# A hybrid trunk's prompt layer summed inside the dense value stage, with paced gathers and another instruction order

## The chip, the cores and the metric

The kernel runs on one core of a Trainium2 chip. The metric is the device time of one execution in microseconds. A core has five engines, each with its own instruction stream: TensorE (PE, matmuls; PEld is its weight loading), VectorE (DVE), ScalarE (ACT), GpSimd (POOL) and SyncE (SP). They meet at semaphores only. SP issues the plain DMA transfers, POOL the indirect ones (gathers of table rows by index).

## What is computed

Two layers over two independent token groups: a prompt of 128 tokens (P, one tile of 128) and a sample of 512 tokens (S, four tiles). Width is 1024, all in float32. Each layer mixes tokens, normalizes, and then passes each token through PEER, a layer of 16384 experts of which every token uses 8 x 16:

```python
def _trunk(x, cvec, lru_state, wkv_state, P):
    for l in range(DEPTH):
        sh1, sc1, g1, sh2, sc2, g2 = _modulation(cvec, w_mod[l], b_mod[l])
        h = _layer_norm(x) * (1.0 + sc1) + sh1
        if l % 2 == 0:
            mix = concat([_fourier_mix(a_in), _short_conv_mix(b_g, c_g, x_in, ...)]) @ w_out_e
        else:
            mix = concat([_lru_mix(...), _rwkv_mix(...)]) @ w_out_o
        x = _layer_norm(ALPHA * x + g1 * mix, ln1)
        h2 = _layer_norm(x) * (1.0 + sc2) + sh2
        x = _layer_norm(ALPHA * x + g2 * _peer(h2, ...), ln2)

def _peer(h, wq, keys, u_tab, v_tab):
    idx, gate = top 16 of 16 x 16 product keys per head, 8 heads
    act = gelu(einsum('td,thkd->thk', h, u_tab[idx]))
    return einsum('thk,thkd->td', gate * act, v_tab[idx])
```

## The kernel before, in words

**The order of the work.** `build` runs layer 0 (`even_mixers`, then `S.peer_layer`) and layer 1 (`odd_mixers`, then `S.peer_layer`). The prompt's work is threaded into these four parts.

**PEER in two ways.** The sample's tiles 1 to 3 go through all 16384 experts as matmuls, in 128 chunks of 128 experts. `hidden` (L1245) multiplies a chunk of u by the tokens and takes the gelu. `dense_peer` (L1255), called the value stage here, multiplies that by the chunk's gates (L1276), splits it into two parts for full precision (`ah` on ACT at L1278, `al` on DVE at L1279), and adds its product with a chunk of v into PSUM (L1285: 18 matmuls a chunk; a chunk of `hidden` has 24, in the helper at L1079). Weight blocks are split likewise (`split`, L1219: the rounded half on ACT, L1222, the rest, `lw`, on DVE, L1224). 64 hidden chunks of a layer are computed ahead and spilled to DRAM while the tiles are routed, so that in the value stage 4 chunks of every 8 are hidden there and 4 are read back. The gates reach DRAM through `one_hot` (L1207) and `scatter_gates` (L1187).

The sample's tile 0 and the prompt's tile go by gathers: for each of 128 slots POOL fetches 128 rows of u (a tile of 512 KB, `gather`, L1145), DVE multiplies and sums them (L1138, a *dot*), then 128 slots of v are fetched and added up (L1168, an *add*). "Sum" below means either. Two tiles, two tables, two layers and 128 slots make 1024 gathers and as many sums.

**The queue.** These gathers are generators in `B.tasks`. `pump(n)` (L199) advances the first of them by n gathers. Others call it as they go: `split` pumps `B.rate`, `one_hot` 1, the value stage enough to be done by chunk 122, less `OVER` = 88 gathers in layer 0, which stay for the odd mixers. `pace(n, src)` (L222) puts a one-column POOL copy of `src` ahead of the gathers it pumps, so that they can't be issued before `src` is there. `defer` (L212) keeps two sums behind the latest gather. Buffers for gathered rows: 4, and 3 more from the pool of the value stage.

**The odd layer.** `odd_mixers` (L1487 and after) starts the sample's `odd_lora` (L608), then `run` (L1378) interleaves generators for the recurrent heads, at most 5 at a time. The prompt's generator first waits until the queue is empty, finishes the prompt's layer 0 (`peer_out`), and only then begins its own mixing (`wkv_inputs`, L719). `end_early` (L467) does the first half of the output projection of layer 1, `end_project` (L495) and `end_steps` (L512) the other half, with `wout` blocks loaded once for each of the tile groups.

**What sets an engine's order.** The program's order is a first order; the tile framework's list scheduler then reorders each engine's stream by priorities, with a modelled timeline of the instructions (`schedule_with_timeline_sim=True`, L1534).

Of the kernel before, what the change touches and what calls it, by code (L numbers as in the profile page):

```python
# [10 lines left out]
F32 = mybir.dt.float32  # L11
# [5 lines left out]
OP = mybir.AluOpType  # L17
# [4 lines left out]
D = 1024  # L22
# [125 lines left out]
class Body:  # L148
    def __init__(self, ctx, tc, I, O):
        self.tc, self.nc, self.I, self.O = tc, tc.nc, I, O  # L150
        E = ctx.enter_context
        self.const = E(tc.tile_pool(name="const", bufs=1))
        self.work = E(tc.tile_pool(name="work", bufs=1))
        self.ps = E(tc.tile_pool(name="ps", bufs=1, space=PSUM))
        self.dram = E(tc.tile_pool(name="dram", bufs=1, space=DRAM))
        self.n, self.md = 0, {}
        self.gp, self.gb, self.gn, self.wb, self.wn, self.rp = None, 0, 0, 0, 0, None
        self.odd, self.tasks, self.pending, self.left = False, [], [], 0
        self.load_constants()
# [52 lines left out]
    def defer(self, *use):  # L212
        self.pending.append(use)
        self.use_gathered(2)

    def use_gathered(self, left=0):
        while len(self.pending) > left:
            f, *a = self.pending.pop(0)
            with self.later(0):
                f(*a)  # L220

    def pace(self, n, src):  # L222
        if self.tasks:
            p = self.tl([128, 1], "pace", 2)
            self.pump(n, self.nc.gpsimd.tensor_copy(p, src[:, 0:1]))
# [95 lines left out]
class Trunk:  # L321
# [54 lines left out]

    def row_of(self, src):
        o = self.B.wide("row", 3)
        self.nc.sync.dma_start(o, src.broadcast_to([128, D]))
        return o  # L380

    def mrow(self, l, v):
        return self.row_of(self.B.md[l, v][self.row:self.row + 1, :])

# [110 lines left out]
    def end_project(self, l, n):  # L495
# [10 lines left out]
        self.todo.append((grp, pts))  # L506

    def end(self, *a):
        for _ in self.end_steps(*a):
            pass  # L510
# [97 lines left out]
    def odd_lora(self, l):  # L608
        nc, T, B, hT = self.nc, self.T, self.B, self.hT
        lo = []  # L610
        for i in range(3):
            z = self.zt()
            self.project(l, "in", hT, 20 + i, z[:, 1:T + 1])
            if self.S:
                B.pace(5, z[:, 1:2])
            o = B.mx([128, T], f"lo{i}" + self.tag)
            self.shift(z, o, 12 + i)
            lo.append(o)
        nc.scalar.activation(lo[0], lo[0], AF.Tanh)
# [99 lines left out]
    def wkv_inputs(self, l, groups, g):  # L719
# [4 lines left out]
        for i in range(3):  # L724
            z = self.zt() if self.S else self.zt("zP", 3)
            if self.S:
                self.project(l, "in", hT, 8 + 4 * i + g, z[:, 1:T + 1])
                self.B.pace(5, z[:, 1:2])
                self.shift(z, z[:, 1:T + 1], 4 * i + g)
                rkv.append([z[:, 1:257], z[:, 257:513]])  # L730
            else:
                z = z.rearrange("p (a b) -> p a b", a=4)
                for hp in range(4):
                    self.project(l, "in", hT, 8 + 4 * i + hp, z[:, hp, 1:T + 1])
                    self.shift(z[:, hp, :], z[:, hp, 1:T + 1], 4 * i + hp)
                rkv.append([z[:, 0:2, 1:T + 1], z[:, 2:4, 1:T + 1]])
            yield
# [585 lines left out]
    def peer_layer(self, l, P):  # L1323
# [3 lines left out]
        with B.tc.tile_pool(name=f"peer{l}", bufs=1, reuse_waits="tile") as self.p:  # L1327
            self.hi, self.lo = [self.tl([128, 8, self.T], n, 1, F32R) for n in ("hi", "lo")]
            with B.tc.tile_pool(name=f"ends{l}", bufs=1, reuse_waits="tile") as B.rp:
                self.end(l, self.hi, self.lo, l == 0 and (lambda: B.modulation(1, 0)))  # L1330
            B.rp = None
            G = B.dram.tile([4 * nd, 128, 128, 32], F32, name=B.name("G"))
            self.scores = B.dram.tile([8, 128, 2, 2, 128], F32, name=B.name("scores"))
            with B.tc.tile_pool(name=f"route{l}", bufs=1, reuse_waits="tile") as self.route_pool:
                self.peer_tiles(l)
                B.rate = 2
                for h in self.route(l, self.groups[0]):
                    pass
                et = self.one_hots(1)
                mine = self.values(0)  # L1340
                B.add(self.dots(0, range(128)), mine, n=256)
                if l == 0:
                    B.add(P.values(0))
                self.spilled = {}
                self.routing = True
                for h in self.route(l, self.groups[1]):
                    self.scatter_gates(G, et, 0, [h])
                    self.spill(l, 3)
                self.routing = False
                for t in (2, 3):  # L1350
                    et = self.one_hots(t)
                    for b in range(8):
                        self.scatter_gates(G, et, t - 1, [b])
                        self.spill(l, 3)
                ges = [self.activated(l, c) for c in range(AHEAD)]
            with B.tc.tile_pool(name=f"dense{l}", bufs=1, reuse_waits="tile") as self.dense_pool:
                B.gp, B.gb, B.rp = self.dense_pool, 3, self.dense_pool
                B.rate, f = 0, {}
                self.dense_peer(l, G, ges, mine, f)
                B.gp, B.gb = None, 0  # L1360
                for grp in (((1, 2), (3,)), ((1,), (2,), (3,)), ((1,), (2, 3)))[1]:
# [12 lines left out]
SPILL = 16  # L1374
LAST, OVER = 122, 88

# [110 lines left out]
def odd_mixers(B, l, P, S):  # L1487
# [6 lines left out]
    def prompt(own, side):  # L1494
        while B.tasks:
            yield
        for _ in range(4):
            yield
        yield from P.peer_out(l - 1)
        B.odd_rate = 3  # L1500
        P.odd_lora(l)
        lru, wkv = [P.odd_lru(l, c) for c in range(4)], list(P.odd_wkv(l))
        n = int(bool(side) and inspect.getgeneratorstate(side[0]) != inspect.GEN_CREATED)
        side[n:n] = lru
        own.extend(wkv)
        yield
# [12 lines left out]

    B.odd, B.odd_rate = True, 6  # L1520
    B.odd_constants()
    S.odd_lora(l)
    lru = [S.odd_lru(l, c) for c in range(4)]
# [17 lines left out]
```

## Time and profile before

| | |
|---|---|
| median of 3 runs | 4570.66 us (4562.15 to 4586.86) |
| the profiled execution | 4558.22 us |
| its span (first to last instruction) | 4556.4 us |
| mean granted TensorE clock | 0.902 |
| busy: PE, PEld, DVE, ACT, POOL | 84%, 69%, 76%, 39%, 30% |
| moved by DMA | 1198 MB, mean 263 GB/s |

Busy shares are averages over stages that differ. The stages, by their first and last instructions in the trace: layer 0's mixers to 430 us, its end and the routing of tiles 0 and 1 to 654, the second group's routing with the scattering of gates to 1023, the value stage of layer 0 from 1023 to 1873, the odd mixers from 1912 to 2940, the end of layer 1's mixers to 3140, routing and scattering to 3643, the value stage of layer 1 to 4498, and the last finish.

### The profile page before, as it was taken

The numbers are of one execution on the slowest core, as the hardware profiler recorded it, in microseconds if no ns is written. First come the engines' busy times: TensorE is split into PE (matmuls) and PEld (weight loads), VectorE is DVE, ScalarE is ACT, GpSimd is POOL, SyncE is SP. The second block draws the span as 40 slices with busy tenths as digits, with TensorE's granted clock in tenths as the row PEclk, the third lists the DMA queues.
The fourth block names the chain that finished last, engine by engine and source line by source line (L and its number), as shares of the span: only waits on it lengthen the run. The fifth ranks groups of instructions, "written<-read, shape, count | busy, mean of one in ns | idle before, by whom it ended". The sixth has DMA issues, their size and how long they took to land. (4 is left out here: it accounts for less than half of the span.)

```text
span 4556.4 us, 71571 instructions
## 1 busy us (share of the span) xinstructions
PE 3837.5 (84%) x26326; PEld 3142.3 (69%) x26326; DVE 3467.4 (76%) x7480; ACT 1757.4 (39%) x3391; POOL 1387.9 (30%) x1105
## 2 busy tenths in 40 slices
PE   7977968999888999778889877719779888988897
PEld 4653767997766788634665654508779877877786
DVE  3398999987889744668554786589999787888845
ACT  2211235763322333244575543203357623332332
POOL 0044322434556200044000232253125354466300
PEclk9997989999999999887888877759999999999999
DMA  9699856999999755368531566487569999999853
GB/s 342 227 350 356 264 196 236 349 357 355 360 360 362 280 175 172 128 237 286 177 101 58 182 222 205 169 289 248 171 225 341 346 367 342 346 365 369 310 170 120
DMA packets 455551, 1198.05 MB, mean 263 GB/s; under 512 B 52848, under 2 KB 195312, under 8 KB 452128
## 3 DMA queue, kind: packets, MB, share of 16 engines
q1 hardware_dynamic: 307744, 656.54, 41.4%
q0 software_dynamic: 147456, 536.94, 32.8%
q8 instruction: 207, 3.39, 0.3%
q14 instruction: 144, 1.18, 0.1%
HBM read 1093.34 MB, written 99.98 MB: 262 GB/s over the span
## 5 line engine op out<-in xcount | busy, mean ns | idle before, releaser
L1079 PE MATMUL ps<-hiS,lwS 128*128 128x384 f32 (+1 forms) x2304 | 817.5, 356 | 81.2 <-DVE lwS L1224 80.9
L1079 PE MATMUL ps<-loS,uhS 128*128 128x384 f32 (+1 forms) x2432 | 857.9, 353 | 1.1 <-DVE loS L432 1.1
L1079 PE MATMUL ps<-hiS,uhS 128*128 128x384 f32 (+1 forms) x2304 | 813.2, 353 | 51.3 <-ACT geS L1252 26.0
L1079 PEld LDWEIGHTS ps<-hiS,lwS 128*128 128x128 f32 x2304 | 447.2, 194 | 111.7 <-DVE lwS L1224 101.4
L1222 ACT ACTIVATE uhS<-w 128x1024 fp32r<-128x1024 f32 x304 | 320.8, 1055 | 527.3 <-PE ps L1079 358.6
L1285 PE MATMUL ps<-vh,ah 128*128 128x512 f32 x1536 | 429.4, 401 | 99.9 <-ACT vh L1222 78.8
L1152 POOL DMA_INDIRECT g<-v,idxP x256 | 351.7, 1374 | 515.8 <-DVE h2P L1168 311.9
L1152 POOL DMA_INDIRECT g<-u,idxS x256 | 349.0, 1363 | 512.9 <-DVE g L1138 391.9
L1079 PEld LDWEIGHTS ps<-hiS,uhS 128*128 128x128 f32 x2304 | 447.5, 194 | 82.3 <-ACT uhS L1222 34.1
L1285 PE MATMUL ps<-lwS,ah 128*128 128x512 f32 x1536 | 483.4, 396 | 10.9 <-DVE lwS L1224 10.8
L1079 PEld LDWEIGHTS ps<-loS,uhS 128*128 128x128 f32 x2432 | 471.5, 194 | 24.0 <-DVE loS L432 3.7
L1285 PE MATMUL ps<-vh,al 128*128 128x512 f32 x1536 | 477.3, 393 | 0.0
L1224 DVE TENSOR_TENSOR lwS<-w,uhS 128x1024 fp32r<-128x1024 f32 x304 | 369.7, 1217 | 122.9 <-ACT uhS L1222 82.0
L1152 POOL DMA_INDIRECT g<-v,idxS x256 | 367.8, 1437 | 237.6 <-DVE h2S L1168 178.6
L1224 DVE TENSOR_TENSOR lwS<-w,vh 128x1024 fp32r<-128x1024 f32 x256 | 312.9, 1223 | 153.7 <-issue 79.3
L1152 POOL DMA_INDIRECT g<-u,idxP x256 | 291.7, 1139 | 414.2 <-DVE g L1138 183.2
L1285 PEld LDWEIGHTS ps<-vh,ah 128*128 128x128 f32 x1536 | 289.1, 192 | 167.1 <-ACT vh L1222 92.5
L1278 ACT ACTIVATE ah<-geS 128x384 fp32r<-128x384 f32 x256 | 134.3, 525 | 671.4 <-PE ps L1285 598.9
L1138 DVE SCALAR_TENSOR_TENSOR g<-g,h2P 128x1024 f32<-128x1024 f32 x256 | 310.2, 1216 | 81.4 <-DMA g<-u,idxP 81.0
L1168 DVE SCALAR_TENSOR_TENSOR h2P<-g,wtP,h2P 128x1024 f32<-128x1024 f32 x254 | 324.6, 1278 | 50.7 <-DMA g<-v,idxP 49.2
L1285 PEld LDWEIGHTS ps<-lwS,ah 128*128 128x128 f32 x1536 | 291.2, 191 | 81.6 <-DVE lwS L1224 20.1
L1285 PEld LDWEIGHTS ps<-vh,al 128*128 128x128 f32 x1536 | 291.4, 190 | 62.8
(480 smaller groups left out, 6687.9 us busy)
## 6 DMA issues: line engine op xcount, KB each, us to landing
w<-ut SPq DMA_DIRECT2D x256, 512.0 KB
w<-v SPq DMA_DIRECT2D x256, 512.0 KB
w<-wblk SPq DMA_DIRECT2D x142, 512.0 KB
w<-wmod SPq DMA_DIRECT2D x96, 512.0 KB
gt<-G SPq DMA_DIRECT2D x64, 768.0 KB
w<-wout SPq DMA_DIRECT2D x56, 512.0 KB
ged<-geS SPq DMA_DIRECT2D x128, 192.0 KB
G<-fa SPq DMA_DIRECT2D x12, 2048.0 KB
```

What stands on the lines that cost most here:

```text
L1079: self.nc.tensor.matmul(out, a[:, s], b[:, k, :], start=k == 0 and i == 0, stop=k == 7 and i == 2)
L1138: self.nc.vector.scalar_tensor_tensor(u, u, 1.0, self.h2[t], OP.mult, OP.mult, accum_out=self.act[t][:, s:s + 1])
L1152: self.nc.gpsimd.indirect_dma_start(out=g, out_offset=None, in_=self.I[tab], in_offset=bass.IndirectOffsetOnAxis(ap=self.idx[t][:, s:s + 1 ...
L1168: nc.vector.scalar_tensor_tensor(acc, v, w[:, s:s + 1], acc, OP.mult, OP.add)
L1222: self.nc.scalar.activation(h, raw, AF.Copy)
L1224: self.nc.vector.tensor_tensor(lo, raw, h.bitcast(F32), op=OP.subtract)
L1278: nc.scalar.activation(ah, ge, AF.Copy)
L1285: nc.tensor.matmul(outs[n][h], a[:, s], b[:, 512 * h:512 * h + 512], start=c == 0 and i == 0, stop=c == 127 and i == 2)
```

## The change

(a) The prompt's adds and finish of layer 0 are queued in `S.peer_layer`, ahead of the sample's dots; nothing of them is left to the odd layer. `split` pumps 1 where it pumped 2 in `peer_layer`. The prompt's odd mixing no longer waits for the queue, begins at once, and yields more often; `odd_rate` goes from 6 to 3.
(b) In the value stage each chunk's gathers stand behind a POOL copy of its multiplied hidden chunk, and are spread evenly; their sums are to come two chunks behind, after `al`. There is one more buffer for gathered rows (4 beside 4) and one more for weights.
(c) In layer 1 `end_tiles` takes the place of `end_steps`: the four remaining `wout` blocks are loaded once, then tile follows tile, with row buffers of 5.
(d) The scheduler's modelled timeline is off.

```diff
-        self.use_gathered(2)
+        self.use_gathered(self.lag)
-    def use_gathered(self, left=0):
-        while len(self.pending) > left:
-            f, *a = self.pending.pop(0)
-            with self.later(0):
+    def use_gathered(self, left=0, after=None):
+        with self.tc.issue_after(after.ins) if after else nullcontext():
+            while len(self.pending) > left:
+                f, *a = self.pending.pop(0)
                 f(*a)
...
+    def end_tiles(self, l, hT, lo):
+        for k in range(self.early, 8):
+            w = B.rp.tile([128, D], F32, name=B.name("wo"), tag="wo", bufs=8 - self.early)
+            nc.sync.dma_start(w, self.I["wout"][l, k])
+            ws.append(w)
...
+        for t in range(self.nt):
+            pts.append([self.pst(*(("pB", 2) if t == 3 else ())) for _ in range(2)])
+            for k in range(self.early, 8):
+                for h in range(2):
+                    nc.tensor.matmul(pts[t][h], self.yT[:, k, t * 128:(t + 1) * 128],
+                                     ws[k - self.early][:, 512 * h:512 * h + 512], start=k == self.early, stop=k == 7)
...
+        self.B.lag, fresh = 5, 0
         for c in range(128):
...
-            elif c < LAST:
-                more = self.B.left - (OVER if l < DEPTH - 1 else 0)
-                self.B.pump(max(0, -(-more // (LAST - c))))
...
-            nc.vector.tensor_tensor(al, ge, ah.bitcast(F32), op=OP.subtract)
+            i = nc.vector.tensor_tensor(al, ge, ah.bitcast(F32), op=OP.subtract)
+            if self.B.lag > 2:
+                self.B.use_gathered(fresh, i)
+            had = len(self.B.pending)
+            if c < LAST:
+                more = self.B.left
+                self.B.pace(min(more, max(2, -(-more // (LAST - c)))), ge)
+            fresh = max(0, len(self.B.pending) - had)
...
-                self.end(l, self.hi, self.lo, l == 0 and (lambda: B.modulation(1, 0)))
+                if self.early:
+                    self.end_tiles(l, self.hi, self.lo)
+                else:
+                    self.end(l, self.hi, self.lo, l == 0 and (lambda: B.modulation(1, 0)))
...
-                B.rate = 2
+                B.rate = 1
+                if l == 0:
+                    B.add(P.values(0))
+                    B.add(P.peer_out(0), n=1)
...
-                if l == 0:
-                    B.add(P.values(0))
...
-                B.gp, B.gb, B.rp = self.dense_pool, 3, self.dense_pool
+                B.gp, B.gb, B.wb, B.rp = self.dense_pool, 4, 1, self.dense_pool
...
     def prompt(own, side):
-        while B.tasks:
-            yield
-        for _ in range(4):
-            yield
-        yield from P.peer_out(l - 1)
-        B.odd_rate = 3
-        P.odd_lora(l)
+        yield from P.odd_lora(l)
...
+        yield from P.wkv_inputs(l, P.inputs, 0)
...
-    with tile.TileContext(nc, schedule_with_timeline_sim=True) as tc:
+    with tile.TileContext(nc, schedule_with_timeline_sim=False) as tc:
```

The order that results on the engines, at three places. First POOL in the value stage of layer 0. Before, a run of the sample's v gathers, with nothing between them:

```order
L1152 DMA g_1967_9340<-v,idxS_710_2899 128x1024
L1152 DMA g_1978_9405<-v,idxS_710_2899 128x1024
L1152 DMA g_1979_9408<-v,idxS_710_2899 128x1024
L1152 DMA g_1990_9473<-v,idxS_710_2899 128x1024
L1152 DMA g_1991_9476<-v,idxS_710_2899 128x1024
```

Now, in the same stage, three u gathers behind each copy (`pace` of `geS`, the multiplied hidden chunk), and at one place in eight chunks several copies in a row with the gathers after them:

```order
L225 COPY pace_2466_11778<-geS_2410_11506 128x1
L1197 DMA g_2467_11780<-u,idxS_710_2899 128x1024
L1197 DMA g_2468_11782<-u,idxS_710_2899 128x1024
L1197 DMA g_2469_11784<-u,idxS_710_2899 128x1024
L225 COPY pace_2476_11821<-geS_2424_11579 128x1
L1197 DMA g_2477_11823<-u,idxS_710_2899 128x1024
L1197 DMA g_2478_11825<-u,idxS_710_2899 128x1024
L1197 DMA g_2479_11827<-u,idxS_710_2899 128x1024
L225 COPY pace_2486_11862<-geS_2438_11652 128x1
L1197 DMA g_2489_11868<-u,idxS_710_2899 128x1024
L225 COPY pace_2496_11905<-geS_2452_11725 128x1
L225 COPY pace_2511_11979<-geS_2463_11769 128x1
```

A gather that could be issued when its buffer was free now also has the copy, and so the hidden chunk, ahead of it.

Second, DVE at the same place. Before: adds of gathered rows (L1168) between the gate multiplication (L1276), the splits (L1224) and `al` (L1279):

```order
L1276 TENSOR_TENSOR geS_2275_10932<-geS_2275_10932,gt_2283_10969 128x384
L1224 TENSOR_TENSOR lwS_2286_10975<-w_2284_10971,uhS_2285_10973 128x1024
L1279 TENSOR_TENSOR al_2302_11074<-geS_2259_10858,ah_2301_11073 128x384
L1168 SCALAR_TENSOR_TENSOR h2S_1870_8844<-g_2282_10966,wtS_1869_8841,h2S_1870_8844 128x1024
L1168 SCALAR_TENSOR_TENSOR h2S_1870_8844<-g_2294_11033,wtS_1869_8841,h2S_1870_8844 128x1024
L1168 SCALAR_TENSOR_TENSOR h2S_1870_8844<-g_2295_11036,wtS_1869_8841,h2S_1870_8844 128x1024
L1276 TENSOR_TENSOR geS_2288_11002<-geS_2288_11002,gt_2332_11243 128x384
```

Now, with L1183 the dots, L1319 the gate multiplication, L1322 `al` and L1269 the splits:

```order
L1319 TENSOR_TENSOR geS_2452_11725<-geS_2452_11725,gt_2462_11767 128x384
L1183 SCALAR_TENSOR_TENSOR g_2477_11823,actS_711_2900<-g_2477_11823,h2S_670_2756 128x1024
L1319 TENSOR_TENSOR geS_2463_11769<-geS_2463_11769,gt_2503_11937 128x384
L1319 TENSOR_TENSOR geS_2473_11811<-geS_2473_11811,gt_2503_11937 128x384
L1322 TENSOR_TENSOR al_2475_11815<-geS_2424_11579,ah_2474_11814 128x384
L1183 SCALAR_TENSOR_TENSOR g_2457_11739,actS_711_2900<-g_2457_11739,h2S_670_2756 128x1024
L1183 SCALAR_TENSOR_TENSOR g_2458_11741,actS_711_2900<-g_2458_11741,h2S_670_2756 128x1024
L1183 SCALAR_TENSOR_TENSOR g_2467_11780,actS_711_2900<-g_2467_11780,h2S_670_2756 128x1024
L1269 TENSOR_TENSOR lwS_2482_11833<-w_2480_11829,vh_2481_11831 128x1024
```

Most sums stand after `al`, in the order of their gathers. One in about every four chunks stands ahead of older ones: here that of g_2477, whose gather comes on POOL behind those of g_2457 to g_2469.

Third, DVE in the odd layer, shortly ahead of the first step of the recurrent scan (`h2P` accumulates the prompt's adds of layer 0; `r`, `h`, `l` belong to the sample's recurrent heads). Before:

```order
L1168 SCALAR_TENSOR_TENSOR h2P_12930<-g_16323,wtP_12927,h2P_12930 128x1024
L698 TENSOR_TENSOR r_3410_16582<-r_3410_16582,r_3412_16584 128x256
L681 SCALAR_TENSOR_TENSOR r_3469_16903<-zl_16237,small,r_3469_16903 128x254
L1168 SCALAR_TENSOR_TENSOR h2P_12930<-g_16326,wtP_12927,h2P_12930 128x1024
L701 SCALAR_TENSOR_TENSOR h_3407_16579<-r_3411_16583,carry_16266,r_3410_16582 128x256
L681 SCALAR_TENSOR_TENSOR r_3469_16903<-zl_16237,small,r_3469_16903 128x253
L965 TENSOR_TENSOR l_3443_16784<-ps_16808,ra_15816 128x2x64
```

Now the prompt's own heads (tiles of 128 columns, `zP`) are in this place:

```order
L893 TENSOR_TENSOR ra_17353<-zP_16258,e_3608_17122 128x256
L894 TENSOR_TENSOR ra_17353<-e_3607_17121,e_3598_17059 128x256
L897 COPY lam_17356<-e_3608_17122 128x4
L899 SCALAR_TENSOR_TENSOR e_3599_17060<-e_3599_17060,e_3630_17305 128x256
L900 TENSOR_TENSOR e_3609_17123<-e_3609_17123,e_3630_17305 128x256
```

The adds of layer 0 are gone from here, and the prompt's mixing has moved up.

## Rows read from the trace of the kernel before

**Rows 1.** The page, part 4: the chain that ended last, by line.

```profile
PE ps L1285 9%; PE ps L1079 5%; DMA w<-v 2%; DVE lwS L1224 0%; DVE h2S L1168 0%; ACT vh L1222 0%; DVE g L1138 0%; ACT ah L1278 0%; DVE tmp L416 0%; DVE half L552 0%; DVE tmp L415 0%; DVE stS L398 0%; DVE tmp L553 0%; DVE geS L1276 0%; ACT u
```

**Rows 2.** Windows: from:to, length, busy us of engines (xinstructions), clock, DMA share, GB/s.

```profile
180.00:430.00 250.00, 188.37 (x764) 116.20 (x762) 216.34 (x630) 37.84 (x78) 85.13 (x80) 0.87 0.88 326
430.00:654.00 224.00, 178.35 (x846) 155.61 (x846) 215.90 (x820) 62.38 (x86) 75.34 (x60) 0.89 0.76 251
654.00:830.00 176.00, 148.25 (x863) 143.18 (x862) 172.99 (x468) 106.15 (x253) 44.87 (x33) 0.93 0.68 241
830.00:1023.00 193.00, 183.57 (x1217) 182.47 (x1215) 163.82 (x199) 141.86 (x350) 82.56 (x57) 0.99 0.96 357
1023.00:1873.00 850.00, 775.93 (x3622) 663.68 (x3623) 603.26 (x720) 271.55 (x367) 282.81 (x204) 0.98 0.81 287
...
1912.00:2165.00 253.00, 185.16 (x1606) 100.21 (x1606) 199.29 (x415) 105.00 (x203) 105.24 (x101) 0.76 0.72 246
2165.00:2940.00 775.00, 638.85 (x9742) 465.87 (x9742) 502.46 (x1602) 383.48 (x848) 116.31 (x148) 0.78 0.48 156
2940.00:3140.00 200.00, 97.11 (x385) 67.63 (x384) 162.21 (x358) 33.06 (x57) 92.98 (x79) 0.73 0.84 289
3140.00:3277.00 137.00, 116.49 (x575) 103.74 (x574) 137.00 (x583) 39.08 (x55) 18.88 (x16) 0.94 0.59 188
3277.00:3411.00 134.00, 106.55 (x607) 100.29 (x607) 131.42 (x395) 81.68 (x198) 22.91 (x14) 0.92 0.56 200
3411.00:3643.00 232.00, 220.75 (x1452) 220.17 (x1450) 196.57 (x173) 164.21 (x406) 105.62 (x60) 0.99 0.94 342
3643.00:4498.00 855.00, 780.23 (x3594) 675.91 (x3595) 653.99 (x850) 269.15 (x361) 355.02 (x252) 0.96 0.88 314
```

**Rows 3.** Chain of waits in value stage 1: start, us, what.

```profile
3715.56 30.06 DMA w<-v x2
...
3909.79 4.12 PE ps L1285 x18
3913.91 4.18 PE ps L1079 x24
```

**Rows 4.** Windows of 16 chunks each in value stage 0.

```profile
1110.00:1220.00 110.00, 102.12 (x477) 87.66 (x475) 92.60 (x115) 33.87 (x47) 58.19 (x43) 0.97 0.97 358
...
1350.00:1480.00 130.00, 107.02 (x491) 88.00 (x490) 119.30 (x133) 37.89 (x51) 79.29 (x58) 1.00 0.98 365
...
1774.00:1873.00 99.00, 99.00 (x481) 87.43 (x480) 46.30 (x56) 36.14 (x48) 0.00 (x0) 1.00 0.52 168
```

**Rows 5.** The same in value stage 1.

```profile
3850.00:3950.00 100.00, 98.59 (x476) 86.85 (x477) 83.94 (x122) 36.37 (x49) 40.42 (x32) 1.00 0.97 345
...
4399.00:4498.00 99.00, 99.00 (x481) 87.41 (x480) 45.94 (x57) 36.00 (x48) 0.00 (x0) 1.00 0.55 175
```

**Rows 6.** Windows of the odd mixers, DVE's adds (L1168) alone.

```profile
1912.00:2165.00 253.00, 103.59 (x81) 0.76 0.72 246
```

**Rows 7.** The same for the dots (L1138; each has a second, short instruction).

```profile
2165.00:2940.00 775.00, 117.73 (x192) 0.78 0.48 156
```

**Rows 8.** Groups of DVE: count, busy us, mean ns, idle before and its releasers.

```profile
L1224 DVE TENSOR_TENSOR lwS<-w,uhS 128x1024 fp32r<-128x1024 f32 x304 | 369.7, 1217 | 122.9 <-ACT uhS L1222 82.0 <-PE ps L1285 38.4 <-PE ps L424 2.2
L1168 DVE SCALAR_TENSOR_TENSOR h2S<-g,wtS,h2S 128x1024 f32<-128x1024 f32 x254 | 325.5, 1281 | 3.2
...
L1138 DVE SCALAR_TENSOR_TENSOR g<-g,h2S 128x1024 f32<-128x1024 f32 x256 | 307.5, 1218 | 18.0 <-DMA g<-u,idxS 18.0
...
L552 DVE TENSOR_TENSOR half<-ps,row 128x512 f32<-128x512 f32 x30 | 20.1, 681 | 27.4 <-DMA w<-wout 17.5 <-PE ps L1285 7.6 <-PE ps L502 2.3
```

**Rows 9.** All gathers (line L1152): issue to landing.

```profile
DMA to landing us min/median/max: 4.1/7.3/14.6
```

**Rows 10.** The pace copies (line L225): ns min/median/max; who waited for them.

```profile
L225 POOL COPY pace<-w x24: 173/184/1003, 2776.9 to 2969.5; 128x1 f32<-128x1 f32 x24
...
  DVE wkm L774: 2.0, 2
```

More of the change, by code (lines that the diff above doesn't have):

```diff
@@ L157, in __init__ @@
         self.gp, self.gb, self.gn, self.wb, self.wn, self.rp = None, 0, 0, 0, 0, None
-        self.odd, self.tasks, self.pending, self.left = False, [], [], 0
+        self.odd, self.tasks, self.pending, self.left, self.lag = False, [], [], 0, 2
         self.load_constants()
@@ L375, in save, with row_of, mrow @@
         self.x[t] = d
-    def row_of(self, src):
-        o = self.B.wide("row", 3)
+    def row_of(self, src, bufs=3):
+        o = self.B.wide("row", bufs)
         self.nc.sync.dma_start(o, src.broadcast_to([128, D]))
         return o
-    def mrow(self, l, v):
-        return self.row_of(self.B.md[l, v][self.row:self.row + 1, :])
+    def mrow(self, l, v, bufs=3):
+        return self.row_of(self.B.md[l, v][self.row:self.row + 1, :], bufs)
     def mcols(self, l, v):
@@ L506, in end_project @@
         self.todo.append((grp, pts))
+    def end_tiles(self, l, hT, lo):
+        nc, B = self.nc, self.B
+        ws = []
+        for k in range(self.early, 8):
+            w = B.rp.tile([128, D], F32, name=B.name("wo"), tag="wo", bufs=8 - self.early)
+            nc.sync.dma_start(w, self.I["wout"][l, k])
+            ws.append(w)
+        self.end_load(l)
+        xs = []
+        for t in range(self.nt):
+            x = self.tmp()
+            nc.sync.dma_start(x, self.x[t])
+            xs.append(x)
+            if t == 1:
+                break
+        g1 = self.mrow(l, 2, 5)
+        g, b = self.row_of(self.I["lnaff"][l, 0:1], 5), self.row_of(self.I["lnaff"][l, 1:2], 5)
+        mc = self.mcols(l, 3)
+        self.h2, self.todo, pts = {}, None, []
+        for t in range(self.nt):
+            pts.append([self.pst(*(("pB", 2) if t == 3 else ())) for _ in range(2)])
[3 more added lines that the diff above has]
+                                     ws[k - self.early][:, 512 * h:512 * h + 512], start=k == self.early, stop=k == 7)
+        for t in range(self.nt):
+            if t < len(xs):
+                x = xs[t]
+            else:
+                x = self.tmp()
+                nc.sync.dma_start(x, self.x[t])
+            self.residual(x, pts[t], g1, 1.0)
+            self.norm([x], g, b)
+            self.save(t, x)
+            self.norm([x])
+            self.transposed([x], (t,), mc, hT, lo)
+            if t not in self.dense:
+                sh2, sc2 = self.mrow(l, 3, 5), self.mrow(l, 4, 5)
+                h2 = self.h2[t] = self.keep([128, D], "h2")
+                nc.vector.scalar_tensor_tensor(h2, sc2, 1.0, x, OP.add, OP.mult)
+                nc.vector.tensor_tensor(h2, h2, sh2, op=OP.add)
     def end(self, *a):
@@ L1329, in peer_layer @@
             with B.tc.tile_pool(name=f"ends{l}", bufs=1, reuse_waits="tile") as B.rp:
-                self.end(l, self.hi, self.lo, l == 0 and (lambda: B.modulation(1, 0)))
+                if self.early:
+                    self.end_tiles(l, self.hi, self.lo)
+                else:
+                    self.end(l, self.hi, self.lo, l == 0 and (lambda: B.modulation(1, 0)))
             B.rp = None
@@ L1518, in prompt @@
             B.add(P.peer_out(l), n=1)
-    B.odd, B.odd_rate = True, 6
+    B.odd, B.odd_rate = True, 3
     B.odd_constants()
-    S.odd_lora(l)
+    for _ in S.odd_lora(l):
+        pass
     lru = [S.odd_lru(l, c) for c in range(4)]
```

9 lines of the change are left out of this document (6 added, 3 removed).

## The prediction

> **What bounds the kernel now.** I read the page's chain first [rows 1]. It is led by TensorE at the two matmul lines, but it reaches back only through the last value stage, so it says nothing of the first 3700 us. For those I cut the span into stages and asked for each engine's busy time in each [rows 2]. The reader is to see that the limit changes from row to row. Where the sample's first tiles are normalized and routed (430 to 830), DVE is busy 215.9 of 224 us and 173.0 of 176 us, and the clock is near full: DVE bounds. In the scattering of gates (830 to 1023) PE is busy 183.6 of 193 us, and the hidden chunks computed there bound. In the odd mixers (1912 to 2940, two rows) no engine is full: PE 185 of 253 and 639 of 775, DVE 199 and 502, with a clock of 0.76 to 0.78. There chains of dependent steps bound, and whatever stands in them.
>
> The two value stages I cut by 16 chunks [rows 4, 5]. Without gathers 16 chunks take 99 us and PE is busy all of it. That is the work itself: 8 hidden chunks of 4.18 us and 16 products of 4.12 us [rows 3] make 99.4. With 32 gathers they take 100, with 43 they take 110, with 58 they take 130 at 365 GB/s and a DMA share of 0.98. So gathers are free up to about 32 per 16 chunks; then each costs (130 - 110) / (58 - 43) = 1.33 us, the time of its 0.524 MB at some 360 to 390 GB/s. Before, they are issued as fast as buffers come free, so a stage begins bound by DMA and ends bound by PE. The chain shows the price in value stage 1: PE stands for 30 us behind two weight blocks [rows 3].
>
> **The change, part by part.** The sum is made against the profiled execution, 4558.2 us. Its span is 1.8 us shorter, and the median of the runs lies 12.4 us higher. The order of the instructions tells how many sums lie where. A dot is 1.22 us with 0.08 for reading its accumulator, an add 1.28, a split 1.22 [rows 8].
>
> *Layer 0 up to the value stage.* Ten more dots fall into the mixers, where DVE is already busy 216 of 250 us: 10 x 1.22 = +12. From 430 to 654 there are 35 sums and 12 splits fewer on the engine that bounds: 35 x 1.22 + 12 x 1.22 = -57. PE's share there also shrinks, so it doesn't catch the gain. From 654 to 830 some 24 sums fewer would be -29; PE's 148 us of 176 leave room for 28, so -28. In the scattering, 11 of those hidden chunks come back on PE: 11 x 4.18 = +46 [rows 3]. Together -27.
>
> *Value stage 0.* It has 204 gathers before and 350 now, because the prompt's 88 adds come here and the sample's dots come later. They stand 3 a chunk up to about chunk 116, 48 per 16 chunks: 110 + 5 x 1.33 = 117 us. 7.25 such groups are 848; the last 12 chunks have few, 12/16 of 99 and a little, 78. So 926 against 850: +76. The lower bound is bytes alone: 850 us at 287 GB/s are 244 MB, 146 more gathers 77 MB, and at 363 GB/s that is 884 us, +34. The upper bound prices each group like the dearest row: 7.25 x 130 + 78 = 1020, +170. I take the row nearest in count (43). The finish of tile 0 now comes behind chunk 116 and not halfway; 12 chunks, 74 us, cover it, and without that cover it would cost about as much as the 39 us that follow the stage now.
>
> *The odd mixers.* 88 adds of the prompt leave. 81 of them stand ahead of the first scan step, 103.6 us of DVE's 199 in that stretch [rows 6]. Against that, the prompt's dots of layer 1 rise from 96 (117.7 us, [rows 7]) to 128, which is +42, and 6 adds are +8: net -62 on DVE. What else counts is that the prompt's mixing no longer waits for the queue: its routing reaches its first one-hot ten scan steps earlier. Which of these sets the end the trace doesn't say, so I bound it. Below: PE's 824 busy us of the 1028, with the start-up that the first row shows as idle PE (253 - 185 = 68), 892, -136. Above: the whole stage at the first row's PE share, 185 / 253 = 0.73, gives 824 / 0.73 = 1128, +100. I take -60, the DVE time net.
>
> *The end of layer 1's mixers.* The blocks of `wout` are loaded at once: the 17.5 us that DVE waits for them go [rows 8]. Seven splits fewer are -9. Together -26; the bound below is the same, above it is 0, as the next thing late is PE's wait for the norm, which stays.
>
> *Routing in layer 1.* Ten sums and 8 splits fewer, 10 x 1.28 + 8 x 1.22 = -23, in the stretch where DVE is full (137 of 137); 15 sums fewer and 4 splits more, -14, in the next; 8 hidden chunks more in the scattering, where PE is busy 221 of 232: +33. Together -4.
>
> *Value stage 1.* It has 252 gathers before, 260 now, evenly 2 a chunk. Eight groups at the 100 us of the row with 32 gathers [rows 5] make 800 against 855: -55. Below, PE's 99 x 8 = 792, -63; above 0.
>
> *The copies.* There are 122 to 124 in each value stage. One takes 0.18 us in the median and 1.0 at most [rows 10], on an engine that is idle half the time; DVE waited 2.0 us for such copies in all. I cost them at nothing; the gathers behind them are wanted two chunks (12 us) later, and land in 7.3 us, at most 14.6 [rows 9]. The Trainium skill (SBUF — State Buffer, "Who interferes with whom") says that a DVE instruction with two SBUF inputs contends with a GpSimd instruction that reads SBUF, and that the second waits until the first has finished. By that rule the sum would be at most 22 us higher, 122 copies of 0.18 us onto a DVE that has little slack in value stage 0; the 2.0 us seen speak against so much.
>
> *The modelled timeline.* Its removal has no row of its own; its effect is in the counts above, which are of the order that results.
>
> Sum: -27 + 76 - 60 - 26 - 4 - 55 = -96, so 4462 on the scale of the profiled execution. On that of the median 12 us are added: **4474 us**, 2.1% faster.
>
> **The rivals.**
>
> *Sums stand too close behind their gathers (slower).* The order puts one sum in about four chunks ahead of older ones, right behind its own gather, and ahead of the gate multiplications and of `al`, on which PE waits. Each would hold DVE for a landing of 7.3 us [rows 9], four in 16 chunks, 29 us. DVE is busy 119 us with 58 sums [rows 4], so 119 - 10 x 1.22 = 107 with 48, and 136 with the waits. Then the stage takes 7.25 x 136 + 78 = 1064, +214 and not +76, and the whole 4600 (4612 on the median's scale), 41 us slower. It decides from 117 + 96 / 7.25 = 130 us per 16 chunks on. For it speaks that DVE is nearly full there; against it, that other sums can be late together with it, and that the hidden chunks are 4 ahead. In value stage 1 DVE has 16 us of slack per group [rows 5].
>
> *The odd mixers don't gain.* The prompt's earlier steps take DVE and PE from the sample's chain, and the order without the modelled timeline puts something in its way. At +0 there the time is 4534, at the bound of +100 it is 4634 (with the 12 us). The middle, +40, is 4574: no change. For it speaks that the added P work (zP rows) stands where the adds stood; against it, that in the first stretch PE is idle 68 us of 253.
>
> *Everything moves beside other work.* The odd stage falls to its PE time (-136) and value stage 0 to its bytes (+34): 4474 - 76 - 42 = 4356. For it speaks the low busy share of all engines in the odd mixers; against it, the 0.76 clock there, by which chains and not work set the time.
>
> **How the numbers follow.** A measurement can tell about 0.5%, 23 us, from no change. My forecast, with its own range of 4410 to 4545, gets 0.45: faster nearly throughout (0.43, same 0.02). Sums too close get 0.18: slower 0.15, same 0.03. The odd mixers without gain get 0.20: 0.07 faster, 0.08 same, 0.05 slower. Everything beside other work gets 0.17, all faster. That is 0.67 faster, 0.13 same, 0.20 slower. The range takes in the last rival and reaches to the slower one: 4345 to 4620, with the far ends of the odd mixers and the dearest stage 0 left out.
>
> **What would show it right or wrong.** Value stage 0 should be about 117 us per 16 chunks to chunk 116, near 360 GB/s throughout, and DVE should hardly wait for a gather; waits of 5 to 10 us there would be the first rival. Value stage 1 should stand at 100 us per 16 chunks with gathers to its end. The odd stage should have no adds of layer 0 and end about 60 us sooner. DVE's wait for `wout` should be gone. The prediction fails if value stage 0 takes over 1000 us, or if the odd mixers take as long as before.

## The result, and the profile after

The changed kernel takes 4621.1 us in the median of four runs (4613.1 to 4641.7), against 4572.2 before (4562.2 to 4586.9): the ratio is 1.0111, with a 95% interval of 1.0067 to 1.0156. It is slower by 1.1%; 4474 was forecast. The profiled execution took 4615.5 us, its span is 4613.7.

First the stages of the changed kernel, busy times by windows as in [rows 2]. The cuts are instructions that both kernels have: the first low part of S's normalized input `hi` (452), the first one-hot (669), the first gate multiplication of a value stage (1112, 3727) and its last, the last scan step (3007).

```profile
100.00:452.00 352.00, 268.04 (x1061) 170.26 (x1059) 191.15 (x567) 45.99 (x94) 69.25 (x68) 0.86 0.74 261
452.00:669.00 217.00, 144.60 (x661) 107.06 (x661) 190.66 (x716) 55.60 (x88) 56.05 (x47) 0.82 0.67 225
...
1112.00:2062.00 950.00, 819.67 (x3700) 698.88 (x3701) 765.13 (x967) 278.00 (x377) 599.11 (x470) 0.93 0.93 340
...
3727.00:4580.00 853.00, 792.36 (x3696) 684.96 (x3697) 660.44 (x860) 280.11 (x375) 467.94 (x380) 0.96 0.90 323
```

The reader is to see three things. DVE is not full between 452 and 669 (191 of 217 us), where it bounded before [rows 2]. Value stage 0 moves 340 GB/s, not the 360 at which gathers set the pace [rows 4]: something else holds it. And the odd stage has become shorter: from the last gate multiplication of layer 0 to the last scan step it takes 946.5 us, and took 1054.4.

Where DVE waits longer shows in its groups, over the whole span, in the columns of [rows 8]. The dots of the prompt wait 155 us for their gathered rows (before 81), those of the sample 57 (before 18.0, [rows 8]), the prompt's adds 83 (before 49). Before, then changed:

```profile
L1138 DVE SCALAR_TENSOR_TENSOR g<-g,h2P 128x1024 f32<-128x1024 f32 x256 | 310.2, 1216 | 81.4 <-DMA g<-u,idxP 81.0
L1168 DVE SCALAR_TENSOR_TENSOR h2P<-g,wtP,h2P 128x1024 f32<-128x1024 f32 x254 | 324.6, 1278 | 50.7 <-DMA g<-v,idxP 49.2
```

```profile
L1213 DVE SCALAR_TENSOR_TENSOR h2P<-g,wtP,h2P 128x1024 f32<-128x1024 f32 x254 | 325.7, 1282 | 83.6 <-DMA g<-v,idxP 82.6
...
L1183 DVE SCALAR_TENSOR_TENSOR g<-g,h2P 128x1024 f32<-128x1024 f32 x256 | 311.0, 1221 | 155.3 <-DMA g<-u,idxP 154.7
...
L1183 DVE SCALAR_TENSOR_TENSOR g<-g,h2S 128x1024 f32<-128x1024 f32 x256 | 303.0, 1220 | 57.2 <-DMA g<-u,idxS 57.0
```

### The profile page after: what moved, and what is told of

Its sections match the earlier page's. It is cut to its first block, busy times and chain, and to the rows that moved or that the text cites. A ratio compares the mean times of both kernels' runs of the same rounds, so it can differ in the third digit from the quotient of the medians.

```text
span 4613.7 us, 71963 instructions
## 1 busy us (share of the span) xinstructions
PE 3828.1 (83%) x26326; PEld 3127.4 (68%) x26326; DVE 3447.2 (75%) x7548; ACT 1761.8 (38%) x3418; POOL 1592.9 (35%) x1317
## 4 chain that ended last, share of the span: by engine, by line
PE 35%; DVE 16%; DMA 16%; issue 7%; ACT 3%; POOL 3%; SPq 0%; DVEq 0%; POOLq 0%; ACTq 0%
PE ps L1335 12%; PE ps L1124 12%; PE ps L438 3%; DMA g<-v,idxP 3%; DMA g<-u,idxP 3%; DMA geS<-ged 3%; DVE lwS L1269 3%; DVE g L1183 2%; POOL g L1197 2%; DMA w<-ut 2%; PE ps L1246 2%; DVE h2S L1213 1%; DVE h2P L1213 1%; DMA g<-u,idxS 1%; DMA w<-v 1%
## 5 line engine op out<-in xcount | busy, mean ns | idle before, releaser
L1124 PE MATMUL ps<-hiS,lwS 128*128 128x384 f32 (+1 forms) x2304 | 801.5, 349 | 37.7 <-DVE lwS L1269 37.6
L1335 PE MATMUL ps<-lwS,ah 128*128 128x512 f32 x1536 | 505.8, 412 | 115.8 <-DVE lwS L1269 115.0
L1335 PE MATMUL ps<-vh,ah 128*128 128x512 f32 x1536 | 482.6, 401 | 53.8 <-ACT ah L1321 27.2
L1269 DVE TENSOR_TENSOR lwS<-w,uhS 128x1024 fp32r<-128x1024 f32 x304 | 370.1, 1222 | 185.4 <-ACT uhS L1267 153.2
L1335 PE MATMUL ps<-vh,al 128*128 128x512 f32 x1536 | 495.7, 405 | 1.6 <-DVE al L1322 1.6
L1197 POOL DMA_INDIRECT g<-v,idxS x256 | 396.4, 1548 | 164.8 <-DVE h2S L1213 106.7
L1183 DVE SCALAR_TENSOR_TENSOR g<-g,h2P 128x1024 f32<-128x1024 f32 x256 | 311.0, 1221 | 155.3 <-DMA g<-u,idxP 154.7
L1197 POOL DMA_INDIRECT g<-u,idxS x256 | 365.1, 1426 | 152.7 <-DVE g L1183 89.5
L225 POOL COPY pace<-geS 128x1 f32<-128x1 f32 x244 | 173.9, 714 | 605.4 <-DVE geS L1319 421.5
L1267 ACT ACTIVATE vh<-w 128x1024 fp32r<-128x1024 f32 x256 | 270.1, 1056 | 211.3 <-DMA w<-v 119.9
L1335 PEld LDWEIGHTS ps<-vh,al 128*128 128x128 f32 x1536 | 302.4, 197 | 70.1 <-DVE al L1322 2.0
```

The lines of the kernel that those rows point to most:

```text
L1124: self.nc.tensor.matmul(out, a[:, s], b[:, k, :], start=k == 0 and i == 0, stop=k == 7 and i == 2)
L1183: self.nc.vector.scalar_tensor_tensor(u, u, 1.0, self.h2[t], OP.mult, OP.mult, accum_out=self.act[t][:, s:s + 1])
L1197: self.nc.gpsimd.indirect_dma_start(out=g, out_offset=None, in_=self.I[tab], in_offset=bass.IndirectOffsetOnAxis(ap=self.idx[t][:, s:s + 1 ...
L1267: self.nc.scalar.activation(h, raw, AF.Copy)
L1269: self.nc.vector.tensor_tensor(lo, raw, h.bitcast(F32), op=OP.subtract)
L1335: nc.tensor.matmul(outs[n][h], a[:, s], b[:, 512 * h:512 * h + 512], start=c == 0 and i == 0, stop=c == 127 and i == 2)
```

## The experiments

The change has four parts: (a) the prompt's layer 0 in value stage 0 and its odd mixing at once, (b) the paced gathers and their sums two chunks behind, (c) `end_tiles` and the copies that pump nothing gone, (d) the modelled timeline off. Ratios are against the kernel before on the same chip, with their 95% intervals; that kernel's median was 4572 to 4578 us there, so a difference of two times from different chips is good to some 6 us at best.

### One part at a time

**d_only:**

```diff
-    with tile.TileContext(nc, schedule_with_timeline_sim=True) as tc:
+    with tile.TileContext(nc, schedule_with_timeline_sim=False) as tc:
```

> Edit: the kernel before with the modelled timeline switched off, nothing else. Theory 1 (the order made without the timeline costs the time: layer 0's mixers +86 us, the scattering +70 and +61 us): about 100 to 200 us slower than before, first hi transposes of layer 0 near 450 us and not 366. Theory 2 (the loss comes from the paced gathers and sums, the timeline is neutral): within 20 us of before, first hi transposes near 366.

Measured: 4808.6 us, ratio 1.0516 (1.0495 to 1.0538). Theory 1 was right in kind and too small in size (231 us, where 100 to 200 was said).

**abc**, the reverse: the changed kernel with that line set back to `True`.

> Edit: the changed kernel with the modelled timeline left on. Theory 1: layer 0's mixers end near 370 us again and the scattering is back near 208 and 193 us, so some 130 to 180 us under the changed kernel's 4621, about 4440 to 4490, faster than before. Theory 2: 4590 to 4630, as the changed kernel.

Measured: 4500.1 us, ratio 0.9829 (0.9809 to 0.9849). Without (d) the change is faster by 1.7%, though 10 us slower than theory 1 gave; (d) costs 121 us on top of the other three.

**a_only, b_only, c_only**: the hunks of one part on the kernel before. In a_only the value stage pumps as before, with nothing left over; in b_only 88 gathers are still left to the odd mixers. (`pace` with n = 0 makes no copy in b_only and c_only, nor in ab below, so (c) on top of ab is `end_tiles` alone.)

> Edit: part (a) alone on the kernel before (the prompt's adds of layer 0 in the value stage, its odd mixing at once, rate 1), gathers pumped as before, timeline on. Theory 1: the odd stage (last gate multiplication of layer 0 to last scan step) falls from 1055 us by 60 to 110, value stage 0 rises from 856 by 60 to 100: net -40 to +20 against before. Theory 2 says the same of this part.

> Edit: part (b) alone on the kernel before (copies ahead of evenly spread gathers, sums two chunks behind, four buffers more and one weight buffer), 88 gathers still left to the odd mixers, timeline on. Theory 1: value stage 1 falls from 866 us to 800 to 830, stage 0 from 856 to about 820 to 850; 20 to 90 us faster. Theory 2: value stage 1 stays near 853 and stage 0 gets no shorter; within 20 us of before, or slower.

> Edit: part (c) alone on the kernel before (the four last wout blocks of layer 1 loaded once, tile by tile; useless copies gone), timeline on. As predicted: 17 to 26 us faster, from the stretch between the last scan step and the first hi transposes (74.5 us before). Rival, from the run of all three parts, where that stretch was 106 us: 20 to 35 us slower there, and no faster in all.

Measured: a_only 4590.7 us, 1.0025 (1.0010 to 1.0040); b_only 4483.2, 0.9805 (0.9787 to 0.9824); c_only 4636.8, 1.0140 (1.0115 to 1.0164). Part (b) carries the gain, (a) gives nothing alone, (c) loses. Part (b) is itself three things, copies with an even spread, more distance to the sums, and two more buffers; they were not tried apart.

**ab and bc**: two parts each.

> Edit: parts (a) and (b) without (c), timeline on. If (c) costs its 30 us at the end of layer 1's mixers: 4465 to 4480, below the 4500 of all three. If (c) is neutral: 4490 to 4510.

> Edit: parts (b) and (c) without (a), timeline on, 88 gathers left to the odd mixers. If (a) costs more in value stage 0 (+70 to 90) than it gives in the odd stage (-45) and the scattering (-11): 4470 to 4500 and no slower than all three parts. If the odd stage needs (a): above 4510.

Measured: ab 4438.1 us, 0.9701 (0.9678 to 0.9724); bc 4527.6, 0.9891 (0.9864 to 0.9917). So (c) costs 62 us on top of (a) and (b), 63 alone, 44 on top of (b). With (b), part (a) gains 45 us (4483 to 4438), which alone it doesn't. By the table below, value stage 0 pays 89 us for (a) alone (943 against 854) and 73 with (b) (894 against 821), so the some 140 sums more that stand there are only a little cheaper where they are paced. The odd mixers gain 45 and 58 us, and value stage 1 loses 10 alone and gains 26 with (b); why was not tried.

The lengths of the stages in microseconds, by the same cuts, from the first and last starts of those instructions in each trace. Each column is one execution; executions of the kernel before took 4559 to 4593 us:

| stage, to | before | changed | d_only | abc | a_only | b_only | c_only | ab |
|---|---|---|---|---|---|---|---|---|
| first hi | 366 | 452 | 457 | 372 | 366 | 371 | 375 | 368 |
| value stage 0 | 657 | 659 | 742 | 645 | 649 | 657 | 665 | 644 |
| its last chunk | 854 | 949 | 835 | 895 | 943 | 821 | 848 | 894 |
| last scan step | 1054 | 947 | 1045 | 1017 | 1009 | 1068 | 1089 | 1010 |
| first hi, layer 1 | 75 | 82 | 81 | 106 | 73 | 75 | 105 | 74 |
| value stage 1 | 637 | 638 | 753 | 619 | 633 | 627 | 676 | 616 |
| its last chunk | 864 | 851 | 845 | 795 | 874 | 809 | 826 | 783 |

### Why (c) loses

The end of layer 1's mixers on DVE, by the timeline, in ab (start, length, instruction, idle before it). The small steps of the normalization follow each other at 0.2 us:

```profile
2977.26 0.16 DVE L405 TENSOR_TENSOR rsS<-rsS 128x2 f32<-128x2 f32 x1
2977.45 0.16 DVE L406 SCALAR_TENSOR_TENSOR rsS<-rsS 128x2 f32<-128x2 f32 x1
2977.65 0.16 DVE L407 SCALAR_TENSOR_TENSOR rsS<-rsS 128x2 f32<-128x2 f32 x1
```

The same steps in abc have one of the prompt's adds between each two, and wait for its rows as well:

```profile
3009.45 0.22 DVE L405 TENSOR_TENSOR rsS<-rsS 128x1 f32<-128x1 f32 x2
3010.04 1.28 DVE L1213 SCALAR_TENSOR_TENSOR h2P<-g,wtP,h2P 128x1024 f32<-128x1024 f32 x1 [0.36 <-DMA g<-v,idxP]
3011.24 0.22 DVE L406 SCALAR_TENSOR_TENSOR rsS<-rsS 128x1 f32<-128x1 f32 x2
3012.63 1.29 DVE L1213 SCALAR_TENSOR_TENSOR h2P<-g,wtP,h2P 128x1024 f32<-128x1024 f32 x1 [1.17 <-DMA g<-v,idxP]
3013.83 0.22 DVE L407 SCALAR_TENSOR_TENSOR rsS<-rsS 128x1 f32<-128x1 f32 x2
```

A step that took 0.2 us takes 1.8 to 2.6. In this stretch abc has 42 adds, ab 7. In ab, 8 POOL copies of `wout` blocks (`pace(1, w)` in `end_project`) keep POOL 63.5 us waiting for those blocks, and the gathers behind them with it; `end_tiles` has no such copy. Two runs take this apart from its working tile by tile. **abc_hold** gives abc a copy of each tile's residual, with two gathers behind it:

```diff
             self.residual(x, pts[t], g1, 1.0)
+            B.pace(2, x)
```

> Edit: the run of all three parts with the timeline on, plus a POOL copy of each tile's residual in end_tiles, with two gathers behind each, so that the gathers and adds that follow in the program wait for the tile. Theory C1 (end_tiles loses because, without the copies that waited for wout, the prompt's adds come into the end of layer 1's mixers: 42 there against 7, each 1.28 us between the small steps of the normalization): the stretch from the last scan step to the first hi falls from 106 us to 75 to 90, the time from 4500 to 4450 to 4480. Theory C2 (tile by tile is itself slower: twice as many small steps): within 15 us of 4500.

**ab_nohold** takes the copies from ab:

```diff
             if self.early:
-                B.pace(1, w)
+                B.pump(1)
```

> Edit: parts (a) and (b), timeline on, with the 8 copies of wout blocks in end_project gone (their gathers pumped without a copy). Theory C1: adds come into the stretch, which grows from 74 to 95 to 110 us; 4438 becomes 4460 to 4500. Theory C2: within 15 us of 4438.

Measured: abc_hold 4433.7 us, 0.9677 (0.9646 to 0.9709), the stretch 65 us with no add in it. ab_nohold 4472.1, 0.9775 (0.9741 to 0.9809), the stretch 89 us with 30 adds. Theory C1 holds both ways: the copies were what kept the adds out. (abc_hold gained more than C1 said, and ab_nohold's stretch grew less, to 89 us and not 95 or more.) With the adds held back `end_tiles` is 9 us shorter in this stretch than `end_steps` (65 against 74); of the whole, abc_hold and ab can't be told apart. The stretch is not all of (c)'s loss: of the 59 us between the two executions of ab and abc it is 32, and of the 78 of c_only 30. Of the rest, the odd mixers and the routing of c_only take 35 and 39 us more and its value stage 1 takes 38 less. Gathers start sooner there too: in the odd mixers abc issues 150 where ab issues 125, c_only 210 where the kernel before issues 184.

### What the timeline gives

In d_only DVE comes to the dots before their rows have landed. These are the waits of DVE from its first one-hot to value stage 0 (total, times, longest):

```profile
DVE g L1138 <- DMA g<-u,idxS: 65.5, 39, 6.2
DVE g L1138 <- DMA g<-u,idxP: 14.0, 9, 4.6
```

In the kernel before, the same stretch has 12.4 us in 6 waits. If distance is what lacks, more sums kept behind the latest gather must help without the timeline and not with it. **after_lag3** and **after_lag4** are the changed kernel (timeline off) with 3 and 4 sums behind outside the value stages, the latter with 5 buffers there and 3, not 4, in the value stages' pool; **ab_lag3** is ab (timeline on) with 3. The line for 3 (the same number is set again behind the value stages):

```diff
-        self.odd, self.tasks, self.pending, self.left, self.lag = False, [], [], 0, 2
+        self.odd, self.tasks, self.pending, self.left, self.lag = False, [], [], 0, 3
...
```

> Edit: the changed kernel, timeline off, with three sums kept behind the latest gather instead of two outside the value stages. If the loss without the timeline is sums that stand right behind their gathers (DVE idle on gathers 155 us for the prompt's dots, 83 for its adds), those waits fall by a third or more and the time falls by 30 to 80 us, to 4540 to 4590. If the loss lies in the rest of the order: within 20 us of 4621.

> Edit: the changed kernel, timeline off, four sums behind the latest gather outside the value stages, with 5 buffers there and 3 in the value stage's pool. If the loss without the timeline is sums too close behind their gathers: DVE idle on gathers falls well under the 260 us of three sums, and the time from 4604 to 4550 to 4585. If most of the loss is the order of the rest (splits, scan, norm): 4590 to 4610.

> Edit: parts (a) and (b), timeline on, with three sums kept behind the latest gather outside the value stages instead of two. If the modelled timeline already places sums behind their landings (DVE idle on gathers is 98 us in all): within 15 us of 4438. If the distance in the program matters with the timeline on too: 4410 to 4425.

| | timeline | us | ratio (interval) | DVE idle until a gathered row |
|---|---|---|---|---|
| changed kernel | off | 4621.1 | 1.0111 (1.0067 to 1.0156) | 303 us |
| after_lag3 | off | 4604.0 | 1.0061 (1.0038 to 1.0083) | 262 |
| after_lag4 | off | 4561.5 | 0.9964 (0.9946 to 0.9983) | 177 |
| abc | on | 4500.1 | 0.9829 (0.9809 to 0.9849) | 147 |
| ab | on | 4438.1 | 0.9701 (0.9678 to 0.9724) | 101 |
| ab_lag3 | on | 4425.1 | 0.9665 (0.9639 to 0.9692) | 99 |

Without the timeline two more sums of distance take 127 us off DVE's waits and 60 off the time, half of what (d) costs. after_lag3 alone, 17 us under the changed kernel, met what was expected if the loss lay in the rest of the order; it takes after_lag4 to show that distance counts. The other half is followed below, and only in part. With the timeline, one more takes off 13 us, and the intervals overlap.

The value stages have their own distance of two chunks. There the changed kernel's order has the sums that stand right ahead of an older one, 29 in the program, and its waits in stage 0 (1112 to 2062) read:

```profile
PE ps L1335 <- DVE lwS L1269: 76.0, 31, 8.7
...
DVE g L1183 <- DMA g<-u,idxS: 41.4, 14, 6.4
```

In abc (1017 to 1912), whose order has 5 such sums, DVE waits 2.9 us for those rows, and PE waits less for splits:

```profile
PE ps L1335 <- DVE lwS L1269: 21.3, 13, 3.1
```

**after_vlag7** takes those sums away with the timeline still off; 4 are left:

```diff
-        self.B.lag, fresh = 5, 0
+        self.B.lag, fresh = 7, 0
```

> Edit: the changed kernel, timeline off; in the value stage no sum is issued while gathers are issued (up to 7 may be open), so every sum comes from the place behind al. In the changed kernel's order 29 sums stand ahead of an older one, here 4. If those sums are what the value stages lose without the timeline (949 and 851 us against 895 and 795): stage 0 falls to 900 to 925, stage 1 to 800 to 830, the whole to 4550 to 4590. If they cost nothing and the rest of the order does it: within 15 us of 4621.

Measured: 4591.0 us, 1.0032 (1.0011 to 1.0054), 30 us under the changed kernel. Stage 0 takes 932 us, stage 1 840; the sample's dots wait 8.7 us instead of 57; PE's wait for splits in stage 0 falls from 76 to 40 us. Both stages stay above what was expected (900 to 925 and 800 to 830). These sums are 28 of the 110 us by which the two stages are longer than in abc; the rest of that order was not tried apart. Two waits of the changed kernel point to it: the multiplications wait 79 us for a spilled chunk in stage 1 (5 in abc), and in stage 0 the loads of spilled chunks wait on SP 131 us for `al` and 30 for the copies to let a buffer go (60 and 11 in abc).

Layer 0's mixers lose 80 us without the timeline. SP, which issues the loads, waits longer there for buffers of weights that modulation matmuls (L300) still hold. In the changed kernel (0 to 452), then in abc (0 to 372):

```profile
SPq L193 <- PE ps L300: 68.0, 28, 11.2
```

```profile
SPq L193 <- PE ps L300: 32.7, 23, 6.3
```

**after_wb3** gives the changed kernel a sixth weight buffer there (`B.wb` of 3, not 2, in `even_mixers`).

> Edit: the changed kernel, timeline off, with 6 weight buffers in layer 0's mixers and not 5. If the mixers lose 80 us without the timeline because weight loads wait for buffers that late modulation matmuls hold (SP waits 65 us for them against 33): the mixers fall from 452 us to 420 to 440 and the time by 10 to 30. If not: within 5 us in the mixers.

Measured: SP's wait for those buffers falls from 68 to 50 us, but the mixers take 453.6 us, as before the edit; refuted. The whole is 4594.2, 1.0050 (1.0028 to 1.0071), from stages that the edit wasn't meant for. **after_nodots** and **abc_nodots** queue none of the prompt's dots of layer 0:

```diff
-            B.add(P.dots(0, range(16 * h, 16 * h + 16)), n=16)
...
+        B.nc.vector.memset(P.act[0], 0.0)
```

> Edit: the changed kernel, timeline off, without the prompt's 128 gathers and dots of layer 0 (their results are left zero). It is read by the stretch up to the first hi transposes alone, beside the same edit with the timeline on. If the prompt's dots are what delays the mixers without the timeline (they stand ahead of the weight splits that PE waits for, 27 us, and DVE waits 48 us for their rows): 452 us falls to 380 to 400, within 25 us of the run with the timeline. If the rest of the order delays them: still 50 us or more apart.

> Edit: the three parts with the timeline on, without the prompt's 128 gathers and dots of layer 0. First hi transposes near 350 to 368 us, against 372 with them, as the modelled order already keeps them out of the way.

Measured, one execution each: the mixers take 422 us without the timeline and 350 with it, 72 apart, against 80 with the dots. So the dots as such are not the cause. But the stretch is not free of sums: with the dots gone, the prompt's adds come forward into it, 39 without the timeline and 23 with it, and DVE waits for their rows, 29 us in after_nodots and 10.5 in abc_nodots:

```profile
DVE h2P L1213 <- DMA g<-v,idxP: 29.0, 19, 4.0
```

So how much of the 72 us hangs on gathered sums stays open, as does which of the rest it is, the modulation, the projections or the prompt's routing. One lead is in the traces: DVE waits 57 us there for an ACT step of the Fourier mix (`y`, L629) in the changed kernel and 49 in after_nodots, but 27 in abc and in abc_nodots.

### A version under both kernels

**hold_lag3** is abc_hold with three sums behind the gathers.

> Edit: all three parts, timeline on, with the copies of each tile's residual in end_tiles that hold the gathers back, and three sums behind the latest gather outside the value stages. If the two gains add: 4434 - 13 = 4415 to 4430, under both kernels and the lowest. If they overlap: 4430 to 4440.

Measured: 4429.7 us, 0.9688 (0.9661 to 0.9716). That is where the two expectations meet; against abc_hold (4433.7, 0.9677) no gain can be told. With ab_lag3 (4425.1, 0.9665) it is the fastest here, and the two can't be told apart: 3% under the kernel before and 4% under the changed one.

## Why the prediction was wrong

The forecast's terms against the same stretches with the timeline on (abc) and in the changed kernel, as differences to the kernel before:

| term | forecast | abc | changed kernel |
|---|---|---|---|
| layer 0 up to the value stage | -27 | -6 | +89 |
| value stage 0 | +76 | +40 | +95 |
| the odd mixers | -60 | -38 | -108 |
| the end of layer 1's mixers | -26 | +32 | +7 |
| routing in layer 1 | -4 | -18 | +1 |
| value stage 1 | -55 | -69 | -13 |
| the rest | 0 | -3 | -14 |
| sum, of the unrounded terms | -96 | -61 | +57 |

**The step that failed** is "The modelled timeline. Its removal has no row of its own; its effect is in the counts above, which are of the order that results." Counts say how many sums stand in a stretch, not how long they wait there. In layer 0's mixers the counts gave +12 for ten more dots, and the stretch grew by 86; without any of the prompt's dots, but with 39 of its adds in their place, it still takes 422 us, where the kernel before takes 366 with 46 dots. By d_only and abc this part alone costs 231 us on the kernel before and 121 on the other three. With it back on, the other terms sum to -61 where -96 was said (by the medians -78). Part of that nearness is luck: they miss by +58 at the end of layer 1's mixers and by +22 and +21 in the odd mixers and in layer 0, and by -36 and -14 in the value stages and -14 in the routing. Nor is the +95 in value stage 0 near the forecast's +76 for its reason; 54 of it came with the timeline's removal.

**The second is "the 17.5 us that DVE waits for them go"**, with "above it is 0". The wait for `wout` went, as foretold, but with it went the copies that waited for the same blocks. I had taken what they hold up for nothing; they held some 35 adds out of a chain of small dependent steps. That term is +32 with the timeline on, and -9 once the gathers are held again. (c) costs about as much again in other stages.

**Value stage 0** was sized from the row with 43 gathers, at 117 us per 16 chunks. In abc it takes +40 at 359 GB/s, near the lower bound of +34 that I gave for bytes alone: with (b) and the timeline on, the gathers there cost about their bytes. With the timeline off the same spread takes 949 us at 340 GB/s, so the spread alone doesn't do it. **Value stage 1** fell by 69 us in abc, where 55 was said; this step was right, and in b_only the stage falls by 55 too.

**The odd mixers** gained more than forecast in the changed kernel (-108) and less with the timeline on (-38). The order without the timeline is shorter there by 70 us, but on the kernel before (d_only) by only 10. Why wasn't tried.

**Of the rivals**, the first came about in kind: sums ahead of older ones made DVE wait 41 us in value stage 0 and 16 in stage 1. It was priced at 29 us per 16 chunks, +138 on the whole; taking these sums away gave 30, of which 28 in the value stages. Few were late by a whole landing: the 14 waits for u rows in stage 0 last 3.0 us in the mean, at most 6.4. The measured time lies near the rival's 4612, but that is luck: only a part of it has the rival's cause. The second rival, that the odd mixers don't gain, was wrong. Of the signs that the prediction named, value stage 0 showed the first rival's (340 GB/s, waits of up to 6.4 us), and the odd stage and the wait for `wout` came as foretold.

## What to carry to other kernels

A switch that changes only the order of instructions has to be priced by waits, and an order has none: undo it alone before any term is trusted. A copy that seems to do nothing can be a gate; ask what stands behind it on its queue, and what that will do when it comes early. A flow of large transfers that is spread evenly over the chunks, with its consumers two chunks behind, can cost little more than its bytes (895 us at 359 GB/s in abc); in another order of the same instructions it did not (949 us at 340 GB/s).

## What was not expected of the hardware

The copies of the multiplied hidden chunk took longer than the copies of [rows 10]: 0.39 us in the median and 4.3 at most, where a copy of a weight block took 0.18. By the source view of the changed kernel (ns min/median/max, then who waited for it):

```profile
L225 POOL COPY pace<-geS x244: 173/393/4328, 1112.3 to 4541.4; 128x1 f32<-128x1 f32 x122
...
  DVE geS L1319: 3.0, 1
```

DVE's own instructions beside them keep their length: an add takes 1.282 us, and took 1.281 [rows 8], a gate multiplication 0.55 in the median. It is POOL that stretches. The Trainium skill (SBUF — State Buffer, "Who interferes with whom") has the second of two instructions block until the first is done, where one is of DVE with two inputs in SBUF and the other of GpSimd and reads SBUF. The trace of the changed kernel agrees for the copies. Of the 244, 167 take over 0.25 us; each of these starts while DVE runs an instruction with two inputs in SBUF that began before it, and ends within 0.05 us of a DVE instruction's end, 0.04 us after it in the median. Of the 77 that take less, 74 start while DVE runs no such instruction. One of the 167, by the timeline; the add ends at 1308.10 and the copy at 1308.14:

```profile
1306.82 1.28 DVE L1213 SCALAR_TENSOR_TENSOR h2P<-g,wtP,h2P 128x1024 f32<-128x1024 f32 x1
...
1307.25 0.89 POOL L225 COPY pace<-geS 128x1 f32<-128x1 f32 x1
```

That they end with DVE's splits (`lwS`) and adds, on whose results they don't depend, speaks against a wait for data. The other way round nothing is seen: the six two-input instructions that began inside a short copy took at most 0.02 us more than the median of their kind. So the 22 us on DVE that the rule could have cost are not there, and DVE waited 3.0 us for the copies in all; it is POOL that pays.
